# Four and then five places for the background rows of the second modulation during attention, and six raw weight rooms for seven

## The chip, the cores and the metric

The kernel runs on one core of a Trainium2 chip. The metric is the device time of one execution in microseconds (us). TensorE (PE) multiplies matrices, VectorE (DVE) and ScalarE (ACT) do the elementwise work, SyncE (SP) issues the transfers (DMA) from the chip's memory.

## The reference

One layer of a decoder trunk on 256 tokens with a model width of 2048, all in fp32:

```python
mod = silu(c) @ w_ada + b_ada
shift1, scale1, gate1, shift2, scale2, gate2 = split(mod, 6)
h = rms_norm(x, norm1_gain) * (1 + scale1) + shift1
x = x + gate1 * mixing_sublayer(h, ...)      # w_in, three kinds of attention, w_br_*, w_out
h = rms_norm(x, norm2_gain) * (1 + scale2) + shift2
x = x + gate2 * swiglu(h, w_ffn_in, w_ffn_out)
```

The mixing sub-layer projects `h` with `w_in` and feeds three branches: stick-breaking attention (6 heads), dilated sliding-window attention (3 groups of 2 heads), and gated linear attention (GLA, 4 heads, chunked). Each branch is projected to the model width, gated, summed and projected with `w_out`. The "second modulation" is `shift2`, `gate1` and `scale2`: each is a vector-matrix product with 2048 x 2048 weights of `w_ada` (`ada_rest` in the kernel), 16.8 MB for each vector. It is needed only after the attention.

## The kernel before, in words

**Weights.** An fp32 product is made of three products of rounded halves (`mm3`: lines L199, L200, L201). Every weight tile (two k-steps by 512 columns, 512 KB) passes through the same four steps. `raw_tile` (L160) takes a free raw room from `free_rooms` and has SP load the tile into it. ACT rounds it to the high half, `whi` (the cast, L189). DVE subtracts to get the low half, `wlo` (the split, L196). PE then does its 12 matmuls, or 6 for half a tile. `whi` and `wlo` have four buffers each, so a cast waits until PE is done with the tile four before it. A raw room is free again when its split is done, and SP's next load into it waits for that.

**Raw rooms.** The kernel starts with `raw0` to `raw3`. In the first group of projections `more_rooms` adds A13, A14 and A15 (seven rooms); `fewer_rooms` takes them away in the third branch's projection, where other tiles join.

**The rows of the second modulation.** These are computed in the background. `ada_segment_steps` issues a load of 128 x 1024 weights (512 KB, L402) into a place of a small ring of tiles (`araw`, `ring["tags"]`), and `mac` (L318, for the first of a row L316) has DVE multiply it by one entry of silu(c) for each partition and add it to `ada`. A `mac` is ordered behind the split that is the latest at that point of the code (`tc.issue_after`). A load waits until the mac that read its place before is done. How often such a step comes is set by `state["rate"]`, a number of steps for each weight tile. The ring has two places, AR0 and AR1, from the start; from `qk_norm(dil_parts)` on it has AR0, AR1, KC and OD (KC holds constants of the attention until their last use), and from `gate_block(0, 1)` on AR0, AR1, KC and KD. `macs` is the list of loads whose mac has not been issued yet.

**Order.** When the program is built, a scheduler sets the order of the instructions on each engine, from dependences, priorities and its own estimate of when each becomes ready. On the chip each engine then works strictly in that order: an instruction that waits holds up all that stand behind it on its engine. So the attention's small steps stand among casts, splits and macs, at places that the scheduler chose.

**Attention.** Stick-breaking (lines L702 to L731) goes head by head: scores on PE (L707, L708), three ACT steps (L710 to L712), DVE (L714, L702), a rounding on ACT (L717), its remainder on DVE (L718), the sums over keys on PE (L723, L724, one pair for the rounded part and one for the remainder), DVE (L725), the exponential on ACT (L727), the mask on DVE (L702), and the product with the values on PE (L730, L731). GLA's end (L862 to L872) multiplies the decayed scores with the values on PE (L866, L867), squares on ACT (L869), forms 1/sqrt of the mean (L299 to L307, on DVE and ACT in turn) and scales on ACT (L872). The dilated attention (L891 on) is mixed at the end (L928 on DVE, L942 on PE).

Of the kernel before, what the change touches and what calls it, by code (L numbers as in the profile page):

```python
# [17 lines left out]
P = 128  # L18
# [3 lines left out]
KC = D // P  # L22
DFF = 5632
NB = 512
# [43 lines left out]
def trunk(ctx: ExitStack, tc: tile.TileContext, I, out):  # L68
# [28 lines left out]
    def misc_bank(shape):  # L97
        return psm.tile(shape, F32, tag="misc", name=nm("misc"))

    @contextmanager  # L100
    def prio(offset=AHEAD):

        with tc.high_priority(offset=offset):
            start = tc.cur_priority
            yield
            n = tc.cur_priority - start
        tc.cur_priority += n
# [63 lines left out]
    def more_rooms(*tags):  # L171
        free_rooms.extend(tags)

    def fewer_rooms(*tags):
        for tag in tags:
            if tag in free_rooms:
                free_rooms.remove(tag)
            else:
                kept_back.add(tag)
# [133 lines left out]
    def ada_mac(acc, raw, k):  # L313
        c = csil[:, k : k + 1]
        if k == 0:
            nc.vector.tensor_scalar(acc, raw, c, None, op0=ALU.mult)  # L316
        else:
            nc.vector.scalar_tensor_tensor(acc, raw, c, acc, op0=ALU.mult, op1=ALU.add)  # L318
# [5 lines left out]
    def ada_group(k0, k1, tags=ADA_TAGS, between=None):  # L324

        n = k1 - k0
        sh, sc = mod1[:, 0, k0:k1], mod1[:, 1, k0:k1]
        count = 0
        pieces = -(-n // 4)
        for i in range(pieces):  # L330
            a = k0 + n * i // pieces
            m = k0 + n * (i + 1) // pieces - a
            w = m * P
            acc = S("ada", [P, 2, w])
            for k in range(KC):
                with prio():
                    raw = S(tags[count % len(tags)], [P, 2, w])
                    nc.sync.dma_start(raw, I[f"ada_{a}_{m}"][k])
                    with tc.issue_after(state["macs_after"]) if "macs_after" in state else nullcontext():
                        ada_mac(acc, raw, k)  # L340
                count += 1
                if k < KC - 1:
                    yield
            if between is not None:
                between()
            with prio():
                c = slice(a - k0, a - k0 + m)
                sums = small([P, 2, m])
                for j in range(2):
                    turned_sums(sums[:, j, :], acc[:, j, :])  # L350
                finish_columns(sums[:, 0, :], sh[:, c], SEG_SHIFT1, a)
                finish_columns(sums[:, 1, :], sc[:, c], SEG_SCALE1, a, ROW_N1)
            yield
        gains[GROUPS.index((k0, k1))] = (sh, sc)
# [19 lines left out]
            g = vec[:, gain_row + k0 : gain_row + k0 + n]  # L374
            state["finish"] = nc.vector.scalar_tensor_tensor(dst, dst, 1.0, g, op0=ALU.add, op1=ALU.mult)

    ring = {"tags": ("AR0", "AR1"), "n": 0}

    def araw(shape, dtype=F32):
        ring["n"] += 1  # L380
        return S(ring["tags"][ring["n"] % len(ring["tags"])], shape, dtype)

    macs = []

    def mac():
        acc, j, k, raw, done = macs.pop(0)
        with tc.issue_after(state["split"].ins):
            ada_mac(acc[j], raw, k)
        if done is not None:
            after.append(done)  # L390

    def ada_segment_steps(acc, seg, done):


        for k in range(KC):
            for j in range(2):
                while len(macs) >= len(ring["tags"]):
                    mac()
                raw = araw([P, 2 * NB])
                c0 = (seg - 2) * D + j * 2 * NB  # L400
                with prio():
                    nc.sync.dma_start(raw, w_ada[k * P : (k + 1) * P, c0 : c0 + 2 * NB])  # L402
                macs.append((acc, j, k, raw, done if (k, j) == (KC - 1, 1) else None))
                yield

    def last_macs():
# [89 lines left out]
    def proj_block(g, b, w=None, carry=False):  # L496
        k0, k1 = GROUPS[g]
        go_on = bool(carried)
        pss = carried.pop() if go_on else [acc_bank() for _ in range(NT)]
        seeded = g == LAST and not go_on  # L500
        if seeded:

            with prio():
                for t in range(NT):
                    nc.scalar.copy(pss[t], A[b][:, t, :])
            go_on = True
        block(pss, h_at, w_in, k0, k1, b, w=w, go_on=go_on, more=carry, seeded=seeded)
        if carry:
            carried.append(pss)
            return  # L510
        with prio():
            first = A[b] is None
            if first:
                A[b] = S(f"A{b}", [P, NT, NB])
            for t in range(NT):
                if first or seeded:
                    nc.scalar.copy(A[b][:, t, :], pss[t])
                else:
                    nc.vector.tensor_add(A[b][:, t, :], A[b][:, t, :], pss[t])
# [3 lines left out]
    def h_group(g):  # L523
        k0, k1 = GROUPS[g]
        sh, sc = gains[g]
        for k in range(k0, k1):
            make_h(k, sh[:, k - k0 : k - k0 + 1], sc[:, k - k0 : k - k0 + 1], g == 0)
# [81 lines left out]
    for g in range(len(GROUPS) - 1):  # L609
        nxt = ada_group(*GROUPS[g + 1])  # L610
        steps = KC * -(-(GROUPS[g + 1][1] - GROUPS[g + 1][0]) // 4)
        done = 0
        for n, b in enumerate(orders[g]):
            while done < (steps * n // (FIN - 1) if g == 0 else steps * (n + 1) // FIN) and next(nxt, "end") != "end":
                done += 1
            if (g, n) == (0, 3):
                more_rooms("A13", "A14", "A15")
            if (g, n) == (0, 6):
                state.pop("casts_after", None)
                state.pop("macs_after", None)  # L620
            proj_block(g, b, early if (g, n) == (0, 0) else None, carry=n == 12)
        for _ in nxt:
            pass
        h_group(g + 1)
# [389 lines left out]
    qk_norm(dil_parts)  # L1014

    state["rate"] = RATE_MID
    ring["tags"] = ("AR0", "AR1", "KC", "OD")

    rr = []
    groups = []  # L1020
# [12 lines left out]
    def gate_block(n, br, steps={}):  # L1033
        pss = [acc_bank() for _ in range(NT)]
        block(pss, h_at, w_in, 0, KC, 15 + 4 * br + n, steps=steps)
        g = S(gtags[n % 2][br], [P, NT, NB])
        with prio():
            for t in range(NT):
                if n == 0:
                    nc.scalar.copy(g[:, t, :], pss[t])  # L1040
                else:
                    nc.scalar.activation(g[:, t, :], pss[t], AF.Sigmoid)
        gates[n, br] = g
# [2 lines left out]
    gate_block(0, 0)  # L1046
    mixture_rows(*groups)
    gate_block(0, 1)
    ring["tags"] = ("AR0", "AR1", "KC", "KD")
    gate_block(0, 2, {2: lambda: od.append(mixture(groups[0]))})  # L1050
    od = od[0]

# [57 lines left out]
    def y_block(n):  # L1110
        y = S("T3", [P, NT, NB])
        for br, (src, kc, act) in enumerate(
            ((I["w_br_sb"], 6, sb_at), (I["w_br_dil"], 2, dil_at), (I["w_br_gla"], 8, gla_at))
        ):
            pss = [misc_bank([P, NB]) if br == 1 else acc_bank() for _ in range(NT)]
            if (n, br) == (3, 2):
                fewer_rooms("A13", "A14", "A15")
                more_rooms("OS0", "OS1", "OS2", "OD")
                state["ordered"] = True
                with_stages(work, pss, act, src, 0, (0, 0, 4, 6, kc), n)  # L1120
            else:
                block(pss, act, src, 0, kc, n)
            with prio():
                for t in range(NT):
                    g = gates[n, br][:, t, :]
                    if br == 0:
                        nc.vector.tensor_mul(y[:, t, :], g, pss[t])
                    else:
                        nc.vector.tensor_mul(g, g, pss[t])
                        nc.vector.tensor_add(y[:, t, :], y[:, t, :], g)  # L1130
        hi = S(ytags[n][0], [P, 4, T], F32R)
        lo = S(ytags[n][1], [P, 4, T], F32R)
        def turn():
            for t in range(NT):
                transpose_split(y[:, t, :], hi, lo, t)

        later.append(turn)
        yT.append((hi, lo))
# [324 lines left out]
    for i in range(NFF):  # L1463
        if i == 0:
# [6 lines left out]
                w_ff, 0, KC, 0, front=("A12", "KD", "AR0", "AR1"), spare=("A9", "A10", "A0", "A1"), behind=order  # L1471
# [154 lines left out]
```

## Time and profile before

| what | before |
|---|---|
| median of 3 runs | 1589.82 us (1589.38 to 1591.12) |
| the profiled execution, its time | 1590.05 us |
| span in its trace | 1588.2 us |
| busy: PE, weight loads of PE, DVE, ACT | 99%, 81%, 84%, 56% |
| memory read | 393.71 MB, 251 GB/s over the span |

The span runs from the first to the last instruction of the trace; the execution has 1.85 us around it. Times in the views below are from the span's start. A row of the timeline gives start, duration, engine, line, operation, output<-inputs, and in brackets how long the engine was idle before it and what released it; `x2` means two instructions in a row. A row of a window gives busy time and instruction count for PE, for PE's weight loads, DVE, ACT and POOL, then the granted clock of TensorE, the busy share of the DMA engines, and GB/s. A row of the waits gives engine, output and line, what was waited for, the total in us, the number of times, and the longest.

### The profile page before, as it was taken

To read this page: it belongs to the slowest core of one execution; us is meant where nothing else is said; L and a number is where in the kernel's file an instruction comes from. 1 tells how busy PE (TensorE), PEld (TensorE's weight loads), DVE (VectorE), ACT (ScalarE), POOL (GpSimd) and SP (SyncE) were. 2 spreads that over 40 slices of the span, in tenths; PEclk is the share of its full clock that TensorE was granted. 3 is DMA by queue.
4 is the path that set the end of the run, shared out by engine and by line. 5 is a ranking of instruction groups with operands and counts; after the bars stand their busy time and mean duration, and the time that the engine had idled before them with its cause. 6 is when DMAs were issued, how large, how long until landed. Compare 5 with 4: busy or idle time off the path is not lost.

```text
span 1588.2 us, 20149 instructions
## 1 busy us (share of the span) xinstructions
PE 1572.1 (99%) x7207; PEld 1292.3 (81%) x7207; DVE 1334.2 (84%) x1513; ACT 893.6 (56%) x1227; POOL 5.3 (0%) x14
## 2 busy tenths in 40 slices
PE   8999999999999999999999999999999999999999
PEld 7878888778878888888888788888888888888887
DVE  6889996787878797879986899999999998877876
ACT  5654448765486444445455756666666665544543
POOL 1000000000000000000000000000000000000000
PEclk9999999999999999999999999999999999999999
DMA  9997987884776998978857665555555647797793
GB/s 334 384 354 279 334 291 252 282 271 148 237 240 211 309 325 291 327 269 298 284 162 244 192 211 199 193 191 198 197 193 209 212 141 247 257 320 254 254 323 138
DMA packets 116181, 399.24 MB, mean 251 GB/s; under 512 B 13091, under 2 KB 13897, under 8 KB 116081
## 3 DMA queue, kind: packets, MB, share of 16 engines
q1 hardware_dynamic: 115856, 397.95, 72.9%
q8 instruction: 56, 0.92, 0.2%
q14 instruction: 45, 0.36, 0.1%
q0 software_dynamic: 224, 0.01, 0.0%
HBM read 393.71 MB, written 4.19 MB: 251 GB/s over the span
## 4 chain that ended last, share of the span: by engine, by line
PE 92%; DVE 4%; DMA 2%; issue 1%; ACT 1%; POOL 0%; DVEq 0%; ACTq 0%; POOLq 0%; SPq 0%
PE acc L201 28%; PE acc L200 28%; PE acc L199 27%; DVE wlo L196 1%; PE misc L201 1%; PE misc L199 1%; PE misc L200 1%; DMA AR<-ada_rest 1%; PE misc L1106 1%; PE acc L461 1%; PE misc L819 1%; DVE ada L318 1%; PE misc L454 0%; ACT whi L189 0%; DMA H<-c 0%
## 5 line engine op out<-in xcount | busy, mean ns | idle before, releaser
L200 PE MATMUL acc<-wlo,H 128*128 128x512 f32 x1398 | 546.9, 391 | 1.1 <-DVE wlo L196 1.0
L201 PE MATMUL acc<-whi,H 128*128 128x512 f32 x1398 | 546.5, 391 | 0.4 <-DVE H L480 0.4
L199 PE MATMUL acc<-whi,H 128*128 128x512 f32 x1398 | 545.2, 392 | 0.5 <-ACT H L473 0.4
L189 ACT CAST whi<-raw 128x1024 fp32r<-128x1024 f32 (+1 forms) x302 | 310.2, 1030 | 317.5 <-PE acc L201 264.4
L196 DVE TENSOR_TENSOR wlo<-raw,whi 128x1024 fp32r<-128x1024 f32 (+1 forms) x302 | 357.6, 1194 | 128.3 <-ACT whi L189 116.4
L189 ACT CAST whi<-A 128x1024 fp32r<-128x1024 f32 (+1 forms) x240 | 248.3, 1036 | 200.3 <-PE acc L201 168.5
L196 DVE TENSOR_TENSOR wlo<-A,whi 128x1024 fp32r<-128x1024 f32 (+1 forms) x240 | 285.5, 1199 | 70.2 <-ACT whi L189 67.0
L200 PEld LDWEIGHTS acc<-wlo,H 128*128 128x128 f32 x1398 | 262.6, 188 | 57.0 <-DVE wlo L196 4.5
L199 PEld LDWEIGHTS acc<-whi,H 128*128 128x128 f32 x1398 | 262.6, 188 | 56.0 <-DVE acc L1240 1.7
L201 PEld LDWEIGHTS acc<-whi,H 128*128 128x128 f32 x1398 | 262.3, 188 | 55.5 <-DVE H L480 1.8
L199 PE MATMUL acc<-whi,A 128*128 128x512 f32 x312 | 122.4, 392 | 0.2 <-DVE acc L1240 0.2
L200 PE MATMUL acc<-wlo,A 128*128 128x512 f32 x312 | 121.6, 390 | 0.1
L201 PE MATMUL acc<-whi,A 128*128 128x512 f32 x292 | 113.9, 390 | 0.0
L199 PEld LDWEIGHTS acc<-whi,A 128*128 128x128 f32 x312 | 58.6, 188 | 13.0 <-DVE acc L1240 1.0
L200 PEld LDWEIGHTS acc<-wlo,A 128*128 128x128 f32 x312 | 58.6, 188 | 12.4 <-DVE wlo L196 0.5
L201 PEld LDWEIGHTS acc<-whi,A 128*128 128x128 f32 x292 | 54.8, 188 | 11.5
L318 DVE SCALAR_TENSOR_TENSOR ada<-AR,csil,ada 128x1024 f32<-128x1024 f32 x39 | 49.8, 1279 | 7.2 <-DMA AR<-ada_rest 7.1
L200 PE MATMUL acc<-wlo,T 128*128 128x512 f32 x120 | 46.7, 389 | 0.0
L201 PE MATMUL acc<-whi,T 128*128 128x512 f32 x120 | 46.7, 389 | 0.0
L199 PE MATMUL acc<-whi,T 128*128 128x512 f32 x120 | 46.7, 390 | 0.0
L201 PE MATMUL acc<-whi,OS 128*128 128x512 f32 x112 | 43.6, 389 | 0.0
L189 ACT CAST whi<-OS 128x1024 fp32r<-128x1024 f32 x30 | 31.7, 1056 | 21.1 <-PE acc L201 17.1
(452 smaller groups left out, 1884.8 us busy)
## 6 DMA issues: line engine op xcount, KB each, us to landing
raw<-w_in SPq DMA_DIRECT2D x118, 512.0 KB, 5.5
A<-w_in SPq DMA_DIRECT2D x85, 512.0 KB, 5.2
raw<-w_ffn_in SPq DMA_DIRECT2D x84, 512.0 KB, 4.6
raw<-w_ffn_out SPq DMA_DIRECT2D x59, 512.0 KB, 5.0
AR<-ada_rest SPq DMA_DIRECT2D x58, 512.0 KB, 5.0
A<-w_ffn_in SPq DMA_DIRECT2D x38, 512.0 KB, 4.6
H<-ada_rest SPq DMA_DIRECT2D x32, 512.0 KB, 5.0
A<-w_ffn_out SPq DMA_DIRECT2D x29, 512.0 KB, 4.8
```

Of the source, the lines that this page charges most:

```text
L189: state["cast"] = nc.scalar.copy(hi, raw)
L196: return nc.vector.tensor_tensor(*args, **kw)
L199: nc.tensor.matmul(ps, lh, rh, start=start, stop=False, skip_group_check=seeded)
L200: nc.tensor.matmul(ps, lh, rl, start=False, stop=False, skip_group_check=seeded)
L201: state["mm"] = nc.tensor.matmul(ps, ll, rh, start=False, stop=stop, skip_group_check=seeded)
L318: nc.vector.scalar_tensor_tensor(acc, raw, c, acc, op0=ALU.mult, op1=ALU.add)
L461: state["warm"] = nc.tensor.matmul(ps, ones_r, wide, start=True, stop=True)
L819: nc.tensor.matmul(ps[:n, t * N_GLA + h, :].rearrange("p (s l) -> p s l", l=L), at(f, h, t)[:, :n], odd(at(f, h, t)), start=True, stop=True,)
L1106: nc.tensor.transpose(ps[:, i, :], src[:, i * P : (i + 1) * P], ident)
```

## The change

The ring of places gets OD and A14 beside AR0 and AR1 from the start of the background rows (four places for two). From `qk_norm(dil_parts)` on it has KC as a fifth, and from `gate_block(0, 1)` on KD in place of OD. A14 is no raw room any more: six rooms for seven from the first group until the third branch's projection. `araw` passes over a place that still holds a load whose mac has not been issued, since places now join a ring that is in use.

```diff
-    ring = {"tags": ("AR0", "AR1"), "n": 0}
+    ring = {"tags": ("AR0", "AR1", "OD", "A14"), "n": 0}
 
     def araw(shape, dtype=F32):
-        ring["n"] += 1
-        return S(ring["tags"][ring["n"] % len(ring["tags"])], shape, dtype)
+        filled = [m[5] for m in macs]
+        while True:
+            ring["n"] += 1
+            tag = ring["tags"][ring["n"] % len(ring["tags"])]
+            if tag not in filled:
+                return tag, S(tag, shape, dtype)
...
-                raw = araw([P, 2 * NB])
+                tag, raw = araw([P, 2 * NB])
...
-                macs.append((acc, j, k, raw, done if (k, j) == (KC - 1, 1) else None))
+                macs.append((acc, j, k, raw, done if (k, j) == (KC - 1, 1) else None, tag))
...
-                more_rooms("A13", "A14", "A15")
+                more_rooms("A13", "A15")
...
-    ring["tags"] = ("AR0", "AR1", "KC", "OD")
+    ring["tags"] = ("AR0", "AR1", "KC", "OD", "A14")
...
-    ring["tags"] = ("AR0", "AR1", "KC", "KD")
+    ring["tags"] = ("AR0", "AR1", "KC", "KD", "A14")
...
-                fewer_rooms("A13", "A14", "A15")
+                fewer_rooms("A13", "A15")
```

The number of loads, macs, casts, splits and matmuls stays the same. What moves is when the ring's loads can be issued, and, since the scheduler orders every engine anew, where the attention's steps stand. In the rows of the changed kernel every line after L376 has a number higher by 4 (L718 is L722, L723 is L727, L866 is L870). A name is followed by numbers of the tile; the tag in front (AR0, OD, A13, raw1, KC) is the place or room.

The first place is the second head of the stick-breaking attention. On DVE, this is what stands from the head's first DVE step (L714, after the change L718) to the remainder L718 (after: L722). Before:

```order
L714 SCALAR_TENSOR_TENSOR scr_603_2652<-misc_601_2645,scr_602_2648 128x384
L196 TENSOR_TENSOR wlo_685_3022<-raw1_683_3019,whi_684_3021 128x512
L702 TENSOR_TENSOR scr_603_2652<-scr_603_2652,KC_486_2176 128x2x128
L720 SCALAR_TENSOR_TENSOR scr_602_2648<-misc_601_2645,scr_602_2648 128x384
L318 SCALAR_TENSOR_TENSOR ada_583_2554<-AR0_673_2966,csil_91,ada_583_2554 128x1024
L318 SCALAR_TENSOR_TENSOR ada_583_2554<-AR1_674_2993,csil_91,ada_583_2554 128x1024
L196 TENSOR_TENSOR wlo_751_3345<-A13_749_3342,whi_750_3344 128x1024
L196 TENSOR_TENSOR wlo_754_3351<-A14_752_3348,whi_753_3350 128x1024
L718 TENSOR_TENSOR T1_604_2655<-scr_603_2652,T1_604_2655 128x384
```

And the same stretch of DVE after the change, with what follows it:

```order
L718 SCALAR_TENSOR_TENSOR scr_603_2652<-misc_601_2645,scr_602_2648 128x384
L706 TENSOR_TENSOR scr_603_2652<-scr_603_2652,KC_486_2176 128x2x128
L196 TENSOR_TENSOR wlo_685_3020<-A15_683_3017,whi_684_3019 128x512
L724 SCALAR_TENSOR_TENSOR scr_602_2648<-misc_601_2645,scr_602_2648 128x384
L722 TENSOR_TENSOR T1_604_2655<-scr_603_2652,T1_604_2655 128x384
L318 SCALAR_TENSOR_TENSOR ada_583_2554<-OD_660_2916,csil_91,ada_583_2554 128x1024
L729 TENSOR_TENSOR scr_602_2648<-scr_602_2648,misc_605_2659 128x384
L318 SCALAR_TENSOR_TENSOR ada_583_2554<-A14_661_2931,csil_91,ada_583_2554 128x1024
L196 TENSOR_TENSOR wlo_751_3343<-raw2_749_3340,whi_750_3342 128x1024
L196 TENSOR_TENSOR wlo_754_3349<-raw3_752_3346,whi_753_3348 128x1024
```

The remainder now stands ahead of the two macs and the two splits that stood ahead of it, and the macs read OD and A14.

On PE at the same head, this is where the pair for the remainder (the second L723, L724 of `misc_605`) stands among the weight matmuls. Before:

```order
L199 MATMUL acc_676_3004<-whi_681_3015,H3_18_115 128x512
L200 MATMUL acc_676_3004<-wlo_682_3016,H3_18_115 128x512
L201 MATMUL acc_676_3004<-whi_681_3015,H7_22_119 128x512
L199 MATMUL acc_675_3003<-whi_684_3021,H3_18_115 128x512
L723 MATMUL misc_605_2659<-T1_604_2655,T3_487_2177 128x384
L724 MATMUL misc_605_2659<-T1_604_2655,ones_r_82 128x128
```

After (both pairs are L727, L728 there):

```order
L199 MATMUL acc_675_3001<-whi_678_3007,H2_17_114 128x512
L200 MATMUL acc_675_3001<-wlo_679_3008,H2_17_114 128x512
L727 MATMUL misc_605_2659<-T1_604_2655,T3_487_2177 128x384
L728 MATMUL misc_605_2659<-T1_604_2655,ones_r_82 128x128
L201 MATMUL acc_675_3001<-whi_678_3007,H6_21_118 128x512
L199 MATMUL acc_676_3002<-whi_678_3007,H2_17_114 128x512
L727 MATMUL misc_605_2659<-T1_604_2655,T3_487_2177 128x384
L728 MATMUL misc_605_2659<-T1_604_2655,ones_r_82 128x128
```

The tiles follow each other as whi_678 (12 matmuls), whi_681 (12), whi_684 (6). The pair stood after the first matmul of whi_684 and stands now after the fourth of whi_678: 12 + 12 + 1 - 4 = 21 weight matmuls earlier. The first pair stands 12 earlier, and the head's L730 has 23 matmuls behind the pair where it had 22.

The second place is the end of GLA, where the third pair of heads is normalised (L299 to L307 on the small tiles `tiny_737` to `tiny_739`; after the change the same tiles). On DVE before:

```order
L196 TENSOR_TENSOR wlo_943_4226<-raw1_941_4223,whi_942_4225 128x1024
L304 TENSOR_TENSOR tiny_731_3286<-tiny_730_3283 128x2
L318 SCALAR_TENSOR_TENSOR ada_583_2554<-KC_874_3840,csil_91,ada_583_2554 128x1024
L305 TENSOR_TENSOR tiny_731_3286<-tiny_731_3286,tiny_729_3281 128x2
L318 SCALAR_TENSOR_TENSOR ada_583_2554<-AR0_900_4002,csil_91,ada_583_2554 128x1024
L196 TENSOR_TENSOR wlo_946_4232<-A13_944_4229,whi_945_4231 128x1024
L306 TENSOR_SCALAR tiny_731_3286<-tiny_731_3286 128x2
L299 TENSOR_SCALAR tiny_737_3304<-tiny_734_3295 128x2
L307 TENSOR_TENSOR tiny_730_3283<-tiny_730_3283,tiny_731_3286 128x2
L196 TENSOR_TENSOR wlo_949_4238<-A14_947_4235,whi_948_4237 128x1024
L304 TENSOR_TENSOR tiny_739_3309<-tiny_738_3306 128x2
L305 TENSOR_TENSOR tiny_739_3309<-tiny_739_3309,tiny_737_3304 128x2
```

On DVE after:

```order
L304 TENSOR_TENSOR tiny_731_3284<-tiny_730_3281 128x2
L318 SCALAR_TENSOR_TENSOR ada_583_2554<-AR1_899_3974,csil_91,ada_583_2554 128x1024
L305 TENSOR_TENSOR tiny_731_3284<-tiny_731_3284,tiny_729_3279 128x2
L318 SCALAR_TENSOR_TENSOR ada_583_2554<-OD_900_4001,csil_91,ada_583_2554 128x1024
L196 TENSOR_TENSOR wlo_955_4249<-raw0_953_4246,whi_954_4248 128x1024
L306 TENSOR_SCALAR tiny_731_3284<-tiny_731_3284 128x2
L299 TENSOR_SCALAR tiny_737_3302<-tiny_734_3293 128x2
L307 TENSOR_TENSOR tiny_730_3281<-tiny_730_3281,tiny_731_3284 128x2
L196 TENSOR_TENSOR wlo_958_4255<-raw1_956_4252,whi_957_4254 128x1024
L304 TENSOR_TENSOR tiny_739_3307<-tiny_738_3304 128x2
L305 TENSOR_TENSOR tiny_739_3307<-tiny_739_3307,tiny_737_3302 128x2
```

The same steps stand three splits later (wlo_955 and wlo_958 for wlo_946 and wlo_949) with the same two macs ahead, which read AR1 and OD in place of KC and AR0. On PE the last L866 of GLA stands 27 rows later than before, with 13 matmuls between it and the last one that reads whi_945, whose buffer whi_957 takes; on ACT, L302, then the L869 that this L866 waits for, stand right behind the cast of whi_957 and an L872.

More of the change, by code (lines that the diff above doesn't have):

```diff
@@ L375, in finish_columns @@
             state["finish"] = nc.vector.scalar_tensor_tensor(dst, dst, 1.0, g, op0=ALU.add, op1=ALU.mult)
-    ring = {"tags": ("AR0", "AR1"), "n": 0}
+    ring = {"tags": ("AR0", "AR1", "OD", "A14"), "n": 0}
     def araw(shape, dtype=F32):
-        ring["n"] += 1
-        return S(ring["tags"][ring["n"] % len(ring["tags"])], shape, dtype)
+        filled = [m[5] for m in macs]
[4 more added lines that the diff above has]
+                return tag, S(tag, shape, dtype)
     macs = []
     def mac():
-        acc, j, k, raw, done = macs.pop(0)
+        acc, j, k, raw, done, _ = macs.pop(0)
         with tc.issue_after(state["split"].ins):
```

## The prediction

> **What bounds the kernel now.** I read the head of the page first, then the chain's shares by engine.
>
> ```profile
> span 1588.2 us, 20149 instructions
> PE 1572.1 (99%) x7207; PEld 1292.3 (81%) x7207; DVE 1334.2 (84%) x1513; ACT 893.6 (56%) x1227; POOL 5.3 (0%) x14
> PE 92%; DVE 4%; DMA 2%; issue 1%; ACT 1%; POOL 0%; DVEq 0%; ACTq 0%; POOLq 0%; SPq 0%
> ```
>
> PE is idle for 1588.2 - 1572.1 = 16.1 us in all. The change leaves every matmul in, so this is all that it can win or add to. Its matmuls follow each other at a pitch read from two rows six matmuls apart: (374.62 - 373.26) / 6 = 0.227 us.
>
> ```profile
> 373.26 0.39 PE L200 MATMUL acc<-wlo,H 128*128 128x512 f32 x1
> ...
> 374.62 0.39 PE L200 MATMUL acc<-wlo,H 128*128 128x512 f32 x1
> ```
>
> Next the stretches of 20 us (PE's busy time is the second number, DVE's the fourth), and PE's own waits.
>
> ```profile
> 60.00:80.00 20.00, 20.00 (x90) 16.56 (x89) 17.04 (x17) 12.84 (x20) 0.00 (x0) 1.00 1.03 405
> 80.00:100.00 20.00, 18.61 (x85) 14.86 (x84) 16.09 (x22) 14.92 (x22) 0.00 (x0) 1.00 0.96 363
> 300.00:320.00 20.00, 17.73 (x81) 14.06 (x80) 18.28 (x23) 13.11 (x22) 0.00 (x0) 1.00 0.86 289
> 420.00:440.00 20.00, 19.41 (x90) 15.84 (x88) 15.14 (x25) 11.63 (x30) 0.00 (x0) 1.00 0.88 293
> 440.00:460.00 20.00, 18.11 (x80) 15.06 (x81) 14.59 (x24) 16.77 (x69) 0.00 (x0) 1.00 0.75 243
> 780.00:800.00 20.00, 19.90 (x91) 16.09 (x91) 19.87 (x21) 12.93 (x14) 0.00 (x0) 1.00 0.56 198
> ```
>
> ```profile
> PE misc L866 <- ACT scr L869: 2.5, 1, 2.5
> PE misc L723 <- DVE T L718: 1.7, 1, 1.7
> PE misc L730 <- DVE scr L702: 0.6, 1, 0.6
> PE misc L942 <- DVE T L928: 0.3, 1, 0.3
> ```
>
> In the attention, PE loses 2.27 us at 300 to 320 (L723 and L730, 1.7 + 0.6) and 1.89 us at 440 to 460, most of it L866's 2.48, which begins at 439.41. The granted clock is 1.00 throughout. What holds DVE there is the ring:
>
> ```profile
> DVE ada L318 <- DMA AR<-ada_rest: 7.1, 5, 2.7
> AR<-ada_rest SPq DMA_DIRECT2D x58, 512.0 KB, 5.0
> SPq L160 <- DVE wlo L196: 611.2, 340, 11.2
> ```
>
> Five macs wait 7.1 us for loads, which take 5.0 us in the middle. The third row is SP waiting for raw rooms; it returns below.
>
> **The change, first place: the second stick-breaking head.** DVE, then ACT, then PE:
>
> ```profile
> 292.97 1.29 DVE L318 SCALAR_TENSOR_TENSOR ada<-AR,csil,ada 128x1024 f32<-128x1024 f32 x1 [0.73 <-DMA AR<-ada_rest]
> ...
> 299.07 1.28 DVE L318 SCALAR_TENSOR_TENSOR ada<-AR,csil,ada 128x1024 f32<-128x1024 f32 x1 [2.69 <-DMA AR<-ada_rest]
> ...
> 302.54 0.55 DVE L714 SCALAR_TENSOR_TENSOR scr<-misc,scr 128x384 f32<-128x384 f32 x1
> ...
> 304.41 2.47 DVE L318 SCALAR_TENSOR_TENSOR ada<-AR,csil,ada 128x1024 f32<-128x1024 f32 x2
> 306.80 2.35 DVE L196 TENSOR_TENSOR wlo<-A,whi 128x1024 fp32r<-128x1024 f32 x2
> 309.07 0.55 DVE L718 TENSOR_TENSOR T<-scr,T 128x384 fp32r<-128x384 f32 x1
> ```
>
> ```profile
> 297.80 0.53 ACT L712 ACTIVATE scr<-scr 128x384 f32<-128x384 f32 x1
> ...
> 300.57 0.62 ACT L189 CAST whi<-raw 128x512 fp32r<-128x512 f32 x1 [1.31 <-PE acc L201]
> 301.25 0.59 ACT L517 COPY A<-acc 128x512 f32<-128x512 f32 x1
> ...
> 304.35 0.51 ACT L717 CAST T<-scr 128x384 fp32r<-128x384 f32 x1
> ```
>
> ```profile
> 304.91 0.44 PE L723 MATMUL misc<-T,T 128*128 128x384 f32 x1
> ...
> 309.68 0.45 PE L723 MATMUL misc<-T,T 128*128 128x384 f32 x1 [1.67 <-DVE T L718]
> ```
>
> With two places, the mac at 292.97 frees its place at 294.2, and the load into it is there at 299.07, 4.8 us later; only one mac stands between. Macs come here at one in about 3 us, so with four places a load has three macs, some 9 us, against 5. I cost the waits 0.73 and 2.69 at nothing: the cover is those three macs, and at two places it is gone again.
>
> Without 2.69, L714 could run at 299.9. Behind it, before L718, stood two macs and two splits (304.41 to 309.07, 4.7 us), now gone to its other side. So DVE alone would start L718 at 309.07 - 2.69 - 4.66 = 301.7. ACT is now the later one: L717 stands behind the 512-wide cast, which waits for PE at 300.57, and behind one copy (to 301.84), so it ends at about 302.35 (301.84 + 0.51), and L718 behind it at 302.9. L712 is no obstacle: one cast more stands ahead of it, and 297.80 + 1.05 + 0.53 = 299.4 is still ahead of L714. PE reached the waiting pair at 309.68 - 1.67 = 308.01 and now reaches it 21 matmuls earlier, at 308.01 - 21 x 0.227 = 303.2, with 0.3 us to spare. The first pair comes 12 matmuls earlier, at 304.91 - 2.72 = 302.2, and finds L717 0.15 late. L730 stands 23 matmuls behind instead of 22. So the wait of 2.27 doesn't go whole: I leave 0.3 for the two. **Term: -2.0**, between 0 (all comes back) and -2.3.
>
> **Second place: the end of GLA.**
>
> ```profile
> 431.04 1.28 DVE L318 SCALAR_TENSOR_TENSOR ada<-KC,csil,ada 128x1024 f32<-128x1024 f32 x1 [0.58 <-DMA KC<-ada_rest]
> 434.05 1.28 DVE L318 SCALAR_TENSOR_TENSOR ada<-AR,csil,ada 128x1024 f32<-128x1024 f32 x1 [1.65 <-DMA AR<-ada_rest]
> ...
> 438.71 1.23 DVE L196 TENSOR_TENSOR wlo<-A,whi 128x1024 fp32r<-128x1024 f32 x1 [1.97 <-ACT whi L189]
> 440.04 0.16 DVE L305 TENSOR_TENSOR tiny<-tiny,tiny 128x2 f32<-128x2 f32 x1
> ```
>
> ```profile
> 437.62 1.06 ACT L189 CAST whi<-A 128x1024 fp32r<-128x1024 f32 x1
> 440.63 0.84 ACT L872 ACTIVATE A<-misc,tiny 128x256 f32<-128x256 f32 x2 [0.56 <-DVE tiny L307]
> 441.36 0.39 ACT L869 ACTIVATE scr<-misc 128x256 f32<-128x256 f32 x1
> 441.89 0.70 PE L866 MATMUL misc<-A,T 128*128 128x256 f32 x2 [2.48 <-ACT scr L869]
> ```
>
> Two macs wait 0.58 + 1.65 = 2.23 us just ahead of the chain L299 to L307; ACT's casts, L872 and L869 stand in order behind that chain, and L866 comes 2.48 late. After the change the macs read places loaded longer ago. What then sets L869 is the cast of whi_957: its buffer comes free 13 matmuls ahead of L866, that is 2.95 us. From cast to the end of L305 the rows take 440.20 - 437.62 = 2.58, then L302 (0.2, as the other small steps) and L869 (0.39): 3.2 us, and some 0.3 for the two hand-overs with PE (the nearest row is 0.28 for L942). So 0.6 of the wait stays. **Term: -1.9**, between 0 (the extra split ahead, 1.15, and a first load into KC that comes late would eat it) and -2.5.
>
> **Third place: the dilated attention's end.**
>
> ```profile
> 490.96 1.01 DVE L928 TENSOR_SCALAR T<-T,dcoef 128x128 f32<-128x128 f32 x4
> 491.39 0.30 PE L942 MATMUL misc<-ident,T 128*128 128x128 f32 x1 [0.28 <-DVE T L928]
> ```
>
> From the last L891 to L942 PE now has 71 weight matmuls where it had 88: 17 x 0.227 = 3.9 us less. DVE has one split (1.15) and two macs (2 x 1.2) less there: 3.5. The wait grows from 0.3 to 0.7. **Term: +0.4**, between -0.3 and +1.
>
> **Other steps.** The other heads stand 8 to 32 matmuls later on PE, each set close to when the scheduler holds it ready, and the head above showed margins of 0.1 to 0.3 us. No row prices this; the nearest are L942's 0.3 and L730's 0.6. **Term: +0.3** for all, one such margin missed, between -0.6 (the loss of 20 - 19.41 = 0.59 at 420 to 440, beside the same waiting macs, goes too) and +2.
>
> **One room less.** SP's 611 us for rooms mean that each load starts when a split ends, so six rooms for seven start a load one split later, and that can cost only where a cast is not already waiting for PE. DMA's share is 0.86, 0.88, 0.75 and 0.56 in the later windows above, and with six rooms some five tiles of 2.7 us of matmuls (12 x 0.227) are under way while a load takes some 5.0 (the ring's row). At 60 to 100 us the share is 1.03 and 0.96: there memory paces the loads, whose order stays, and with 1.03 PE still has 20.00 of 20. I take **0**, between 0 and +1.4, one more gap like that of 80 to 100 (20 - 18.61 = 1.39).
>
> **The late macs.** The last two macs of scale2 come some thirty splits later, into 780 to 800, where DVE is busy for 19.87 of 20 while PE has 19.90. Nothing is added in total; **0**, between -0.3 and +0.5.
>
> **Sum:** -2.0 - 1.9 + 0.4 + 0.3 = -3.2 us. The profiled execution took 1590.05 (span 1588.2 and 1.85 around it), so a like one would take 1586.85. It lies 0.23 above the median of 1589.82, so I forecast 1589.82 - 3.2 = **1586.6 us**.
>
> By the Trainium skill, "DMA: Bandwidth & Descriptors", section on the anatomy of one DMA, a transfer costs about 2.0 us plus its bytes at 436 GB/s (fitted on GpSimd's path): my estimate from that is 3.2 us for 512 KB. The wait of 2.69 would then have been 1.1 and the one of 1.65 nothing, so the places would have had little to give. The trace disagrees: 4.8 us here and 5.0 in the group, on SP's queue; the measurement decides.
>
> **The rivals.**
>
> *Only the first wait goes.* GLA's end is set by DVE's own work: six macs and four splits stand ahead of the chain there, where five and three did. That is 2.35 us more, against 2.23 of waits gone. Against it: the chain also starts later on PE, by about 27 matmuls. Then -2.0 + 0.8 = -1.2: **1588.6**.
>
> *Nothing is won.* PE is busy for 99%, and an order made anew puts the steps as close as they were, so that new waits of the size of L730's 0.6, five of them, replace the large ones: **1589.8**. For it: margins of 0.1 to 0.3. Against: the large waits came from loads, which such an order did not foresee. The Trainium skill, "Perfetto Trace Analysis", section "Identifying the Most-Contended Engine", has one optimize the engine of the highest occupancy, and judge TensorE by its weight loads (81% here). The change takes no work from TensorE; by that rule alone the time would stay.
>
> *Slower: the lost room.* In the first 100 us the rooms run against a memory that is full (1.03, 0.96). If a landing comes after PE has freed the cast's buffer, PE loses what it is late. A gap of 1.39 us is there already. More than two further gaps eat the gain of 3.2, and five (7.0) make it slower by over 0.2%: **1593.6**. It decides when SP's issues fall more than the slack, about one split and cast (2.2 us), behind. Against it: 20.00 of 20 at 60 to 80.
>
> **How the numbers follow.** 0.2% is 3.2 us, about what a measurement of this kernel tells from no change, so faster means below 1586.64 and slower above 1593.0. Forecast (both waits mostly go): 0.58, with a range of its own from 1584.4 (the four listed waits, 5.1 us, go whole, and 0.3 of the small ones) to 1588.0. The forecast lies on the bound; since the loss at 420 to 440 is not in the sum and would go the same way, I put 0.36 at faster and 0.22 at same. Only the first: 0.16, same. Nothing won: 0.17, of which 0.04 faster, if the new order falls well, and 0.13 same. The lost room: 0.09, slower. Together faster 0.40, same 0.51, slower 0.09. The range takes in the forecast, the first two rivals and the +0.5 of the late macs above no change: 1584.4 to 1590.3. It leaves out the lost room and, at the ends of the other cases, about another tenth.
>
> **What the changed profile would show.** Right: no wait of DVE's L318 for AR over 1 us between 270 and 440; PE's waits at the second head (L727, L734 there) under 0.5, at L870 about 0.6, at L946 about 0.7; 300 to 320 with PE above 19.5. Wrong: L870 still over 2 behind DVE (first rival); several new waits of PE on DVE or ACT between 240 and 500 (second); PE below 19 in a second stretch between 60 and 240, with splits waiting for `raw` loads (third). What would make it wrong that I can't see: KC's first load, which must wait for the last masked copy of GLA, and the order of the GLA heads, which all moved.

## The result, and the profile after

The changed kernel takes 1585.61 us (median of 7 runs, 1585.34 to 1586.57); the kernel before, run beside it again, 1591.12 (7 runs, 1589.38 to 1592.46). The ratio is 0.997, with a 95% interval of 0.9959 to 0.998: 3.2 to 6.5 us faster, 5.5 between the medians. The spans of the two traces differ by 1588.2 - 1583.8 = 4.4 us; the profiled execution of the kernel before (1590.05) is itself some 1 us below that median. The forecast was 3.2 us less, 1586.6.

The head of the page after, and the chain's shares:

```profile
span 1583.8 us, 20157 instructions
PE 1572.0 (99%) x7207; PEld 1292.4 (82%) x7207; DVE 1334.7 (84%) x1513; ACT 893.9 (56%) x1227; POOL 5.3 (0%) x14
PE 96%; DVE 3%; issue 1%; ACT 1%; DMA 0%; ACTq 0%; DVEq 0%
```

All busy times are those of before to within 0.5 us. What went is idle time of PE, 16.1 to 11.8 us, and DMA's share of the chain went from 2% to 0%. The stretches of 20 us show where. First the one row of before that was not shown, then those of after:

```profile
800.00:820.00 20.00, 19.73 (x95) 15.92 (x94) 19.39 (x22) 10.95 (x14) 0.00 (x0) 1.00 0.66 224
```

```profile
300.00:320.00 20.00, 20.00 (x93) 16.23 (x91) 19.65 (x26) 16.09 (x28) 0.00 (x0) 1.00 0.95 329
420.00:440.00 20.00, 20.00 (x103) 16.43 (x103) 18.01 (x28) 11.30 (x30) 0.00 (x0) 1.00 0.83 263
440.00:460.00 20.00, 20.00 (x90) 16.55 (x89) 14.85 (x22) 18.55 (x71) 0.00 (x0) 1.00 0.95 346
780.00:800.00 20.00, 19.73 (x86) 15.69 (x85) 19.93 (x21) 13.35 (x14) 0.00 (x0) 1.00 0.51 165
800.00:820.00 20.00, 19.31 (x97) 15.73 (x96) 19.06 (x22) 11.12 (x14) 0.00 (x0) 1.00 0.65 217
```

PE wins 20.00 - 17.73 = 2.27 us at the stick-breaking heads and (20 - 19.41) + (20 - 18.11) = 2.48 at GLA's end, and loses 0.17 + 0.42 = 0.59 more at 780 to 820. The 2.48 is the whole of L866's wait, which lay across the border of two stretches (439.41 to 441.89). Some 0.5 more lies in the first 20 us, where PE was busy for 17.01 before and 17.52 after; that stretch came out anywhere from 16.54 to 17.49 in the other traces, whatever the kernel, so I don't count it for the change.

At the second head (L722 is the remainder, L727 the two waiting pairs of before), DVE, then PE:

```profile
301.26 0.55 DVE L724 SCALAR_TENSOR_TENSOR scr<-misc,scr 128x384 f32<-128x384 f32 x1
301.72 0.55 DVE L722 TENSOR_TENSOR T<-scr,T 128x384 fp32r<-128x384 f32 x1
302.19 1.28 DVE L318 SCALAR_TENSOR_TENSOR ada<-OD,csil,ada 128x1024 f32<-128x1024 f32 x1
```

```profile
301.66 0.45 PE L727 MATMUL misc<-T,T 128*128 128x384 f32 x1
...
302.52 0.34 PE L727 MATMUL misc<-T,T 128*128 128x384 f32 x1
```

The remainder is done at 302.27 and PE comes for it at 302.52. No mac waits here. PE's remaining waits in the attention and behind it:

```profile
PE misc L365 <- DVE ada L318: 0.7, 1, 0.7
PE misc L946 <- DVE T L932: 0.3, 1, 0.3
```

### The profile page after: what moved, and what is told of

It reads as the page before. It is cut to its first block, busy times and chain, and to the rows that moved or that the text cites. A ratio compares the mean times of both kernels' runs of the same rounds, so it can differ in the third digit from the quotient of the medians.

```text
span 1583.8 us, 20157 instructions
## 1 busy us (share of the span) xinstructions
PE 1572.0 (99%) x7207; PEld 1292.4 (82%) x7207; DVE 1334.7 (84%) x1513; ACT 893.9 (56%) x1227; POOL 5.3 (0%) x14
## 4 chain that ended last, share of the span: by engine, by line
PE 96%; DVE 3%; issue 1%; ACT 1%; DMA 0%; ACTq 0%; DVEq 0%
PE acc L201 29%; PE acc L200 29%; PE acc L199 28%; PE acc L465 1%; DVE wlo L196 1%; PE misc L199 1%; PE misc L201 1%; PE misc L200 1%; PE misc L1110 1%; PE misc L823 1%; PE misc L458 0%; PE misc L365 0%; PE misc L686 0%; PE misc L871 0%; PE misc L727 0%
## 5 line engine op out<-in xcount | busy, mean ns | idle before, releaser
L189 ACT CAST whi<-raw 128x1024 fp32r<-128x1024 f32 (+1 forms) x326 | 335.0, 1031 | 337.3 <-PE acc L201 295.7
L196 DVE TENSOR_TENSOR wlo<-raw,whi 128x1024 fp32r<-128x1024 f32 (+1 forms) x326 | 386.5, 1196 | 121.4 <-ACT whi L189 115.6
L196 DVE TENSOR_TENSOR wlo<-A,whi 128x1024 fp32r<-128x1024 f32 x216 | 257.0, 1199 | 79.2 <-ACT whi L189 75.7
L189 ACT CAST whi<-A 128x1024 fp32r<-128x1024 f32 x216 | 223.3, 1036 | 176.4 <-PE acc L201 154.9
L318 DVE SCALAR_TENSOR_TENSOR ada<-H,csil,ada 128x1024 f32<-128x1024 f32 x30 | 37.5, 1279 | 0.7 <-DMA H<-ada_rest 0.7
```

The costliest lines, as they stand in the source:

```text
L189: state["cast"] = nc.scalar.copy(hi, raw)
L196: return nc.vector.tensor_tensor(*args, **kw)
```

## The experiments

Two theories stood at the start. Theory 1, the prediction's: the places keep loads ahead of their macs, and that alone frees DVE and then PE. Theory 2: the room that is gone makes the scheduler order the attention anew, and the order alone does it.

**Four places at the start only.** Of the changed kernel, the two later rings are put back:

```diff
-    ring["tags"] = ("AR0", "AR1", "KC", "OD", "A14")
+    ring["tags"] = ("AR0", "AR1", "KC", "OD")
...
-    ring["tags"] = ("AR0", "AR1", "KC", "KD", "A14")
+    ring["tags"] = ("AR0", "AR1", "KC", "KD")
```

> The changed kernel, but from the third group of projections' end (qk_norm(dil_parts)) on the ring has four places as before (AR0, AR1, KC, OD, then AR0, AR1, KC, KD); A14 is still no raw room. Theory 1 (depth: a mac waits less for its load where the ring has more places): the stick-breaking heads keep the gain (PE over 19.9 of 20 at 300 to 320), the fifth place's part is lost: PE waits at GLA's end 1 to 2.5 us again behind DVE's macs; span 1585 to 1586.5. Theory 2 (order: the room that is missing makes the scheduler order the attention anew, and that alone moved the small steps out of harm's way): no wait at GLA's end, since the last product of GLA stands 27 matmuls later on PE here too; span about 1583.3, the changed kernel's 1583.8 less 0.5 of the late macs, which are back in their old place.

Measured: 1586.11 us, ratio to before 0.9971 (0.996 to 0.9982), span 1583.7. PE is busy for 20.00 at 300 to 320 and for 20.00 at 440 to 460 too. Theory 1 missed the second half: the fifth place isn't needed at GLA's end.

**Five places later only**, two until then:

```diff
-    ring = {"tags": ("AR0", "AR1", "OD", "A14"), "n": 0}
+    ring = {"tags": ("AR0", "AR1"), "n": 0}
```

> The changed kernel, but with two places (AR0, AR1) until qk_norm(dil_parts), five from there. Theory 1: DVE's macs wait some 4 to 5 us for AR loads between 270 and 330 again, and PE loses 1 to 2.3 us in the stick-breaking heads; GLA's end stays free; span 1585 to 1586. Theory 2: the first four positions of L727 on PE are within 3 of the changed kernel's, so its gain stays: PE over 19.9 at 300 to 320, span 1583.8.

Measured: 1590.77, ratio 1.0006 (0.9996 to 1.0015), span 1588.6: nothing is left of the gain. At 300 to 320 PE is busy for 20.00, as theory 2 said: the new order alone frees the second head. But later heads wait in its place (18.81 at 320 to 340, 18.24 at 360 to 380), and even GLA's end, with five places and six rooms, isn't free (19.20 at 440 to 460). PE's waits:

```profile
PE misc L734 <- DVE scr L706: 1.8, 1, 1.8
PE misc L727 <- DVE T L722: 1.2, 1, 1.2
...
PE misc L870 <- ACT scr L873: 0.8, 1, 0.8
```

The wait of L727 stands behind a mac that waits 1.30 for AR at 331.48. The largest, L734's, does not: DVE waits there in L747, the first step of GLA, for ACT's cast of another load, `in_a`.

```profile
362.68 0.41 ACT L746 CAST T<-scr 128x256 fp32r<-128x256 f32 x1 [2.57 <-DMA scr<-in_a]
363.12 0.43 DVE L747 TENSOR_TENSOR T<-scr,T 128x256 fp32r<-128x256 f32 x1 [1.49 <-ACT T L746]
```

SP issued that load at 357.23 here and at 350.13 in the changed kernel. Whether the two places are what makes it late was not tested.

**One room less, the ring untouched.** In the kernel before:

```diff
-                more_rooms("A13", "A14", "A15")
+                more_rooms("A13", "A15")
...
-                fewer_rooms("A13", "A14", "A15")
+                fewer_rooms("A13", "A15")
```

> The kernel before with one raw room less (A13, A15), the ring untouched. Theory 1: both waits of PE stay in some form (macs wait 5 us or more for loads), span 1586.5 to 1588.5; no loss to the room. Theory 2: span about 1583.3 to 1584, no wait of PE over 0.5 in the attention. Third theory (the lost room costs PE where memory is full): PE loses over 1 us more than 1.39 between 60 and 240.

Measured: 1588.84, ratio 0.9991 (0.9983 to 1.0), span 1586.5. Five stretches of it:

```profile
80.00:100.00 20.00, 18.60 (x85) 14.87 (x84) 16.11 (x22) 14.92 (x22) 0.00 (x0) 1.00 0.92 345
300.00:320.00 20.00, 20.00 (x93) 16.13 (x92) 17.81 (x24) 15.36 (x27) 0.00 (x0) 1.00 0.87 285
320.00:340.00 20.00, 18.66 (x85) 14.88 (x84) 17.36 (x20) 11.73 (x18) 0.00 (x0) 1.00 0.89 312
360.00:380.00 20.00, 18.13 (x104) 14.41 (x103) 7.86 (x13) 11.27 (x19) 0.00 (x0) 1.00 0.44 136
440.00:460.00 20.00, 20.00 (x90) 16.57 (x89) 14.94 (x25) 18.49 (x71) 0.00 (x0) 1.00 0.85 287
```

The lost room costs nothing where memory is full (18.60 against 18.61), so that theory falls. GLA's wait is gone with the order alone, as theory 2 said. At the heads the loss has only moved to later ones, and has grown: 1.34 and 1.87 us where the kernel before lost 2.27. Both places, on DVE and on PE:

```profile
331.79 1.29 DVE L318 SCALAR_TENSOR_TENSOR ada<-AR,csil,ada 128x1024 f32<-128x1024 f32 x1 [1.49 <-DMA AR<-ada_rest]
...
338.39 0.55 DVE L718 TENSOR_TENSOR T<-scr,T 128x384 fp32r<-128x384 f32 x1
...
357.44 1.28 DVE L318 SCALAR_TENSOR_TENSOR ada<-AR,csil,ada 128x1024 f32<-128x1024 f32 x1 [1.95 <-DMA AR<-ada_rest]
```

```profile
339.00 0.44 PE L723 MATMUL misc<-T,T 128*128 128x384 f32 x1 [1.34 <-DVE T L718]
...
361.71 0.44 PE L723 MATMUL misc<-T,T 128*128 128x384 f32 x1 [1.08 <-ACT T L717]
```

A mac waits 1.49 for AR, the remainder L718 stands behind it, and PE waits 1.34. At 361.71 PE waits 1.08 for ACT's L717, which waits for DVE's steps behind the mac of 357.44, itself 1.95 late. So over all the heads theory 1 holds, and at GLA's end theory 2. The next run tells them apart from the other side.

**A third place, all seven rooms.** The kernel before with this one line:

```diff
-    ring = {"tags": ("AR0", "AR1"), "n": 0}
+    ring = {"tags": ("AR0", "AR1", "OD"), "n": 0}
```

(`araw` as in the changed kernel.)

> The kernel before with one place more, AR0, AR1 and OD until qk_norm(dil_parts), and all seven raw rooms; from there the ring of before. GLA's last products stand on PE as in the kernel before (the last one three matmuls later), so here the place is told from the room. If the third place is enough for the stick-breaking heads (a load then has two macs, some 6 us, against 5), their 2.3 us go: PE over 19.9 at 300 to 320. GLA's end: if the missing room's order took its wait away, the 2.5 us stay here, span 1585.9; if the places did, they are gone here too, span 1583.5.

Measured: 1585.67, ratio 0.9968 (0.9955 to 0.998), span 1584.1. The heads are free: PE is busy for 19.96 at 300 to 320. At GLA's end, DVE, ACT (L873 is before's L869, L876 its L872) and PE (L870 is L866):

```profile
431.45 1.28 DVE L318 SCALAR_TENSOR_TENSOR ada<-AR,csil,ada 128x1024 f32<-128x1024 f32 x1 [2.05 <-DMA AR<-ada_rest]
...
435.20 1.28 DVE L318 SCALAR_TENSOR_TENSOR ada<-KC,csil,ada 128x1024 f32<-128x1024 f32 x1 [1.05 <-DMA KC<-ada_rest]
```

```profile
437.37 0.40 ACT L873 ACTIVATE scr<-misc 128x256 f32<-128x256 f32 x1
...
439.45 0.84 ACT L876 ACTIVATE A<-misc,tiny 128x256 f32<-128x256 f32 x2 [0.66 <-DVE tiny L307]
```

```profile
437.92 0.70 PE L870 MATMUL misc<-A,T 128*128 128x256 f32 x2 [0.16 <-ACT scr L873]
...
456.91 0.44 PE L686 MATMUL misc<-ident,A 128*128 128x128 f32 x2 [0.59 <-DVE A L674]
```

DVE waits 3.10 us for loads there, more than the 2.23 of before, and PE 0.16 where it waited 2.48. Another 0.59 follows 19 us later, where PE finds DVE late at the next stage's norm; in the kernel before nothing waits there. What differs is ACT's order: the square L873 stands ahead of the scaling L876, which waits for DVE's chain. In the kernel before it stood behind it (440.63 L872, then 441.36 L869). In the changed kernel it stands ahead of the third pair's L876 as well:

```profile
439.76 1.05 ACT L189 CAST whi<-raw 128x1024 fp32r<-128x1024 f32 x1
440.71 0.83 ACT L876 ACTIVATE A<-misc,tiny 128x256 f32<-128x256 f32 x2
441.44 0.20 ACT L302 ACTIVATE tiny<-tiny 128x2 f32<-128x2 f32 x1
441.53 0.38 ACT L873 ACTIVATE scr<-misc 128x256 f32<-128x256 f32 x1
...
443.43 0.83 ACT L876 ACTIVATE A<-misc,tiny 128x256 f32<-128x256 f32 x2
```

**That order by hand.** In the kernel before, GLA's second half keeps the first pair's normalisation back until both pairs are squared:

```diff
+            squared = []
             for h2 in range(2):
...
-                r = rsqrt(ss, 1.0 / T, [P, 2])
-                for i in range(2):
+                squared.append((h2, ps, ss))
+                if t == 1 and h2 == 0:
+                    continue
+                for h2, ps, ss in squared:
+                  r = rsqrt(ss, 1.0 / T, [P, 2])
+                  for i in range(2):
                     nc.scalar.activation(o[:, 2 * h2 + i, :], ps[:, i, :], AF.Copy, scale=r[:, i : i + 1])
+                if t == 0:
+                    squared = []
```

> The kernel before (two, then four places, seven rooms), but in GLA's second half the squares of both pairs of heads are written ahead of the two normalisations, so that on ACT the L869 on which the last L866 waits stands ahead of the third pair's L872 and not behind it. DVE's order is that of before up to the third pair's L304, so its macs wait for the same loads. Theory A (what cost 2.48 us at GLA's end is that ACT's square stood behind a scaling that waits for DVE; the loads only set how late that was): the wait of L866 goes to under 0.5 although DVE still waits about 2 us for loads at 430 to 435; PE's 2.27 at 300 to 320 stays; span about 1586.0. Theory B (the loads' wait must go for PE's wait to go): PE loses 1 to 2.5 us at GLA's end as before, span 1587.5 to 1588.2.

Measured: 1589.52, ratio 0.9992 (0.9983 to 1.0001), span 1587.9. The wait of the last L866 (here L867) is gone, with a mac still waiting 1.51 at 434.34. But 1.56 of the 2.48 come back 19 us later than its old place, where the next stage's norm finds DVE late. And the second head, whose order is that of before, loses more than before: a mac waits 4.46 there where it waited 2.69, and PE is busy for 16.62 at 300 to 320 (17.73 before).

```profile
300.38 1.28 DVE L318 SCALAR_TENSOR_TENSOR ada<-AR,csil,ada 128x1024 f32<-128x1024 f32 x1 [4.46 <-DMA AR<-ada_rest]
...
434.34 1.28 DVE L318 SCALAR_TENSOR_TENSOR ada<-AR,csil,ada 128x1024 f32<-128x1024 f32 x1 [1.51 <-DMA AR<-ada_rest]
```

```profile
460.69 0.77 PE L682 MATMUL misc<-ident,A 128*128 128x128 f32 x4 [1.56 <-DVE A L670]
```

So theory A is shown for L866's wait and missed on the span, both by what came back and by the loads of the second head. The loads wait 1.51 at GLA's end here where they waited 2.23, which by itself would take 0.7 of the 2.48 away. This kernel also moved that L866 28 places ahead on PE, so the square's place isn't the only difference.

**The loads in pieces of 512 bytes**, in the kernel before and in the changed one, every engine's order kept:

```diff
-                    nc.sync.dma_start(raw, w_ada[k * P : (k + 1) * P, c0 : c0 + 2 * NB])
+                    rows = w_ada[k * P : (k + 1) * P, c0 : c0 + 2 * NB]
+                    if seg != SEG_GATE2:
+                        full = w_ada[k * P : (k + 1) * P, (seg - 2) * D : (seg - 1) * D]
+                        nc.sync.dma_start(
+                            raw.rearrange("p (b c) -> p b c", c=P),
+                            full.rearrange("p (b a c) -> p a b c", a=2, c=P)[:, j],
+                        )
+                    else:
+                        nc.sync.dma_start(raw, rows)
```

> The kernel before with every instruction in its old order, but the background loads of shift2, gate1 and scale2 are fetched in pieces of 512 bytes (every second block of 128 columns) where they were 4 KB in a row: the same bytes, slower on the way, and the columns of these three rows come out permuted. If the loads are what the two waits hang on, DVE's waits for AR loads grow from 7.1 us to well over 10, and PE's waits at L723 (1.7) and L866 (2.5) each grow by about what a load takes longer than 4.8 us, a few us slower in all. If it's only the order of the small steps, they stay where they are, within 0.3 us, and so does the span of 1588.2.

> The changed kernel with its order kept and the same loads in pieces of 512 bytes (the columns of the three rows permuted). With four places a load has some 9 us before its mac. Theory 1 (depth covers the loads): as long as a load stays under about 9 us, no wait of PE over 0.5 comes at the stick-breaking heads or at GLA's end, and the span stays within 0.5 of 1583.8. If depth is not what covers, it loses as much as the kernel before does with the same loads.

Measured: 1590.52, ratio 0.9998 (0.9988 to 1.0008), span 1589.2, and 1586.46, ratio 0.9978 (0.9969 to 0.9987), span 1585.9. The loads hardly got slower: the median for AR went from 5.0 to 5.1 us in the kernel before and from 5.0 to 5.3 in the changed one, and other runs with whole rows have 4.9 to 5.4. So the pair doesn't test what slower loads would do to four places, and that part stays open. The changed kernel's span is not within 0.5 of 1583.8: it is 2.1 longer. But PE waits neither at the heads nor at GLA's end; the loss lies before 20 us (0.95) and behind 1540 (1.3). The pair shows something else, since single loads fell differently in the kernel before, under an order that is the same instruction by instruction (lines 8 higher: L738 is L730, L874 is L866):

```profile
311.59 1.28 DVE L318 SCALAR_TENSOR_TENSOR ada<-AR,csil,ada 128x1024 f32<-128x1024 f32 x1 [2.11 <-DMA AR<-ada_rest]
...
431.84 1.28 DVE L318 SCALAR_TENSOR_TENSOR ada<-KC,csil,ada 128x1024 f32<-128x1024 f32 x1 [0.44 <-DMA KC<-ada_rest]
433.92 1.28 DVE L318 SCALAR_TENSOR_TENSOR ada<-AR,csil,ada 128x1024 f32<-128x1024 f32 x1 [0.73 <-DMA AR<-ada_rest]
```

```profile
316.76 0.67 PE L738 MATMUL misc<-scr,A 128*128 128x256 f32 x2 [1.66 <-DVE scr L710]
441.77 0.70 PE L874 MATMUL misc<-A,T 128*128 128x256 f32 x2 [1.44 <-ACT scr L877]
```

At the head, the mac ahead waits 2.11 where it waited 1.06 in the profile of before (+1.05), and PE's L730 waits 1.66 where it waited 0.6 (+1.06). At GLA's end the two macs wait 1.17 where they waited 2.23 (-1.06), and PE's L866 waits 1.44 where it waited 2.48 (-1.04). At these two waits of the old order PE pays each microsecond of the loads one for one. It isn't so at every wait: at the mac ahead of the remainder the loads wait 2.43 for 2.69 (-0.26) and PE 1.58 for 1.67 (-0.09).

**All traces together.** What the macs waited for loads at the heads (270 to 400 us), and how long PE was idle there (280 to 400), by the number of places up to `qk_norm(dil_parts)`:

| places | trace | macs wait for AR | PE idle |
|---|---|---|---|
| 2 | the kernel before | 5.5 | 2.27 |
| 2 | five places later only | 2.5 | 2.94 |
| 2 | one room less | 4.3 | 3.21 |
| 2 | the squares' order by hand | 7.2 | 3.38 |
| 2 | the kernel before, 512-byte pieces | 6.8 | 3.24 |
| 3 | a third place | 0 | 0.06 |
| 4 | the changed kernel (two traces), its start alone, its 512-byte pieces, and the next run (two traces) | 0 | 0.00 to 0.12 |

With three places or more no mac waits for AR at the heads. On PE these traces have two orders of the heads with two places (the second and third row share one) and two with more. What was not run is one order kept while only the number of places changes: each number made the scheduler set the order anew.

**Four places at the end.** The changed kernel with this line:

```diff
-    ring["tags"] = ("AR0", "AR1", "KC", "KD", "A14")
+    ring["tags"] = ("AR0", "AR1", "KC", "KD")
```

> The changed kernel, but from gate_block(0, 1) on four places (AR0, AR1, KC, KD) as before, so that the last two macs of scale2 stand behind splits 255 and 273 again and not 285 and 287. If these two macs cost the 0.6 us that PE loses more at 780 to 820 in the changed kernel (19.73 + 19.31 against 19.90 + 19.73), it comes back: span 1583.2. If that loss has to do with something else, the span stays at 1583.8.

Measured: 1585.69, ratio 0.997 (0.9959 to 0.9981), span 1582.9. First what waits there in the changed kernel, then the late stretches of this run:

```profile
803.54 1.28 DVE L318 SCALAR_TENSOR_TENSOR ada<-KC,csil,ada 128x1024 f32<-128x1024 f32 x1
```

```profile
804.96 0.74 PE L365 MATMUL misc<-ident,ada 128*128 128x128 f32 x5 [0.69 <-DVE ada L318]
```

```profile
780.00:800.00 20.00, 19.89 (x92) 16.13 (x91) 19.87 (x22) 13.48 (x15) 0.00 (x0) 1.00 0.48 152
800.00:820.00 20.00, 19.74 (x93) 15.95 (x92) 19.41 (x22) 11.51 (x15) 0.00 (x0) 1.00 0.63 214
```

With the fifth place, one of the last macs of scale2 comes at 803.54, right ahead of L365, which turns `ada` on PE. Without it the 0.59 us come back (19.89 + 19.74 against 19.73 + 19.31). The medians (1585.69 and 1585.61, from two chips) don't show so little, so both kernels ran once more on one chip:

> The changed kernel with four places from gate_block(0, 1) on, once more beside the changed kernel on one chip: if the two late macs cost 0.6 us, this one is 0.5 to 1 us below the changed kernel in the span and in the median; if not, the two agree within 0.3.

> The changed kernel itself, beside the run with four places at the end on the same chip. Span 1583.8 within 0.7 (the first 20 us alone moved by 0.5 to 1 between runs), PE's loss at 780 to 820 0.96 us again.

Measured: 1585.06 (1584.72 to 1585.63), ratio 0.9964 (0.9951 to 0.9978), span 1582.9; the changed kernel 1586.18 (1585.85 to 1587.82), ratio 0.9973 (0.9963 to 0.9984), span 1584.3. The runs of the two don't overlap here: four places at the end are the better version, by 1.1 us between these medians and by 0.9 between the first traces. The late macs are not all of it: the 0.59 come back in both traces, but at 860 to 900 both lose some 0.2 against the changed kernel, and what else makes up the difference was not followed.

## Why the prediction was right, and where it was not

- **First place, -2.0: -2.27 measured, mechanism right.** Macs waited for loads, DVE's small steps stood behind them, and PE behind those. With two places macs wait for loads in all five traces, 2.5 to 7.2 us, and PE loses 2.3 to 3.4 us at the heads; with three or four, under seven rooms and under six, no mac waits for AR there and PE loses at most 0.1. The second head alone came free in two traces with two places, by order; the loss then stood at later heads, and not all of it behind macs (L734's 1.76). The margin was forecast as 0.3 and is 0.25; the 0.3 left for the first pair and L730 was too much, since ACT's L721 was done at 301.6 as PE came for it.
- **Second place, -1.9: -2.48 measured, right in sign, the cause at best half told.** The step that failed is "What then sets L869 is the cast of whi_957". I let L302 wait for L305; it needs only L301 before it, on ACT, so the split and L304, L305 are not in that chain. From the start of that cast to the end of the square it took 2.15 us (439.76 to 441.91) and not 3.2, PE came at 442.51, and the 0.6 that I left did not come. And the step before it, that the wait goes because "the macs read places loaded longer ago", isn't needed. The macs just ahead of the chain do wait no more in the changed kernel. But the new order also takes the square out from behind the third pair's scaling, and with that, in the kernel with a third place, 3.1 us of waiting for loads cost PE 0.16 there, and 0.59 at the next stage's norm. Loads did set the size of the wait in the old order, one for one; by that, ending their 2.23 alone would leave some 0.25 of the 2.48, an estimate that no run checks. So two things changed that may each end this wait, and the prediction has the square at its new place but credits the loads alone: that its size came near is in part luck. The prediction also counted one thing twice: it took the 0.59 lost at 420 to 440 for a loss of its own, not in the sum, and raised the chance of faster for it. It is the first part of L866's 2.48, which begins at 439.41. That the fifth place is not needed there was shown; the exact share of room and place in making the new order wasn't told apart, since either alone (six rooms, or three places) gave one.
- **Third place, +0.4: 0.0.** L946 still waits 0.3. Why the seventeen matmuls less didn't show was not followed up.
- **Other steps, +0.3: none.** No new wait of PE over 0.3 stands in the attention. Waits like those of the rival in which nothing is won did appear (1.8, 1.2 and 0.8), but only with two places at the start.
- **One room less, 0: right for memory** (18.60 against 18.61), but not neutral: alone it makes the scheduler order the attention anew and takes 1.7 us off the span: GLA's 2.48 less, some 0.9 more at the heads. The medians of that run leave it open (0.9983 to 1.0).
- **Late macs, 0: +0.59, just outside the +0.5 I allowed.** "Nothing is added in total" held for DVE; what I didn't follow is who waits for the last of these macs: L365 on PE.

The terms that missed are -0.27, -0.58, -0.4, -0.3 and +0.59, together -0.96; the two traces differ by another 0.2 or so, within the start's spread. So the sum of -3.2 came out at -4.4 between the traces, and at -5.5 between the medians, with an interval of -3.2 to -6.5: the forecast lies at its small end. The forecast time is nearer to the measured one, 1.0 off, since its base of 1589.82, from three runs, was 1.3 below the median of seven. And faster, which it was, had been given 0.40, less than the 0.51 for no change.

The Trainium skill ("Perfetto Trace Analysis", "Identifying the Most-Contended Engine") has one optimize the engine of the highest occupancy first. One rival read it as no change here, since PE gets no less work. PE's busy time is indeed the same to 0.1 us, but the gain is all in its 16 us of gaps.

## What to carry to other kernels

A background load whose consumer stands in an in-order queue ahead of urgent steps needs enough buffers for its whole latency: here two were not enough for 5 us at a step every 3 us, three were. Where a small step on one engine waits behind another that waits for a second engine, its place in the queue can be worth more than the speed of what it waits for (PE waited 0.16 for 2.48 us here, with longer waits for loads). And when buffers are added to the end of a background job, look at who needs its last result: a deeper ring also finished later here, and cost 0.59 us.

## What the runs showed of the hardware that I had not expected

Loads of 128 x 1024 in pieces of 512 bytes took 5.1 us in the middle where rows of 4 KB took 5.0 (AR, the kernel before). I had expected a clear difference; the medians of the runs with whole rows alone spread from 4.9 to 5.4.
